# Hybrid two-layer block, FP32 by split products: block products by seven in the first feed-forward matrix instead of the second

## The chip, the cores and the metric

The kernel runs on one core of a Trainium2 chip. The metric is the device time of one execution in microseconds (us). Three runs of the kernel before stand beside one profiled execution, which the hardware recorded instruction by instruction. The engines are TensorE (PE, with PEld for its weight loads), VectorE (DVE), ScalarE (ACT), GpSimd (POOL) and SyncE (SP), which issues the DMAs.

## The reference

A sequence of 256 tokens of width 1024 goes through two layers. Each layer is feed-forward, mixer, feed-forward, each followed by a residual and a layer norm. The mixer of layer 0 is a hybrid of a gated delta rule and a state-space scan, that of layer 1 a sparse attention; neither is touched by the change. The part that matters, four times in all:

```python
D_MODEL, SEQ, D_FF = 1024, 256, 2816

def swiglu(x, w_in, w_out):
    gate, up = jnp.split(x @ w_in, 2, axis=-1)      # w_in 1024 x 5632
    return (jax.nn.silu(gate) * up) @ w_out         # w_out 2816 x 1024

h = layer_norm(DEEPNORM_ALPHA * h + 0.5 * swiglu(h, ffn_w_in[layer, 0], ffn_w_out[layer, 0]),
               ln_g[layer, 0], ln_b[layer, 0])
```

All is float32.

## The kernel before

**Split products.** Every float32 operand of the large products is split into a high part and a low part (`split`, `hard_split`): ACT copies it rounded (`whi`, `fhi`, `g`), DVE subtracts that from the source (`wlo`, `flo`). A product is then three: high by high, high by low, low by high (`mm3`). Each weight is loaded once from HBM, in raw tiles of 128 x 2048 (1 MB, four buffers, `RAW = 4`), split into halves of 128 x 1024, and used once, since all 256 tokens fit in one pass. Everything in fast memory besides the raw tiles, the tokens and small constants comes from one pool of 36 tiles of 128 x 1024 (`m4`), shared by streams with quotas: "W" for split weights, "G" for gated activations, "F" for sums, "L" for the residual.

**A feed-forward** (`ffn`) goes through its 2816 features in 11 steps of 256. Steps 0 and 1 compute tokens by features and transpose the result (`pair_weights`, `proj_tok`). Steps 2 to 10 are ordinary: for each 128 features, `proj_two` multiplies 8 blocks of the weights' high part by the tokens' high and low parts side by side (8 matmuls of 512 columns), and 8 of the low part by the high one (8 of 256), for the gate and again for the up half; `add_two` adds the two sides, ACT takes silu, DVE multiplies, and the gated block is split into `g`. In the program such matmuls read `ps<-x,whi` and `ps<-x,wlo`. The second matrix adds each block of 128 features into four PSUM banks (`acc`, two token blocks by two column halves): 12 matmuls of 512 columns, `out_mm`.

**Seven for eight, before.** For steps 4 to 7 (`SEVEN = (4, 8)`) the second matrix is done by a scheme with seven block products in place of eight (a Strassen-Winograd form). Two blocks of 128 features and two token blocks give the sums of activations (`token_forms`, tiles `F`, `fhi`, `flo`), two feature blocks and two column halves those of weights (`weight_forms`, tiles `t13`, `t24`), and seven products of 128 x 128 by 128 x 512, each three matmuls, go into banks which are combined at the end into the residual (`put`, tiles `u`). The gated blocks of steps 8 to 10 then go through `out_mm` for the first token block, and, while its layer norm runs on DVE, for the second (`late`).

**The order.** Nothing is issued as written. `Plan` records all operations; `order` schedules them as a list with prices and latencies written in the class, program order as priority, tiles handed out when a buffer is free, and the program emits what results: one fixed queue for each engine. In a feed-forward the copies to high parts are fixed to ACT (`self.hard`). Since every operation is issued from one place, all lines of the profile read L540, and groups are told apart by the names of tiles.

Of the kernel before, what the change touches and what calls it, by code (L numbers as in the profile page):

```python
# [18 lines left out]
P = 128  # L19
# [14 lines left out]

QUOTAS = {"M": None, "D": None, "F": None, "S": (8, 8), "Z": (4, 4), "L": (4, 4), "G": (20, 20), "P": (5, 5), "Q": (5, 5), "W": (12, 24)}

# [14 lines left out]
SEVEN = (4, 8)  # L51
# [512 lines left out]
class K:  # L564
# [3 lines left out]
    def __init__(self, plan, ins, caps):  # L568
        self.nc = self.plan = plan
        self.i = ins  # L570
        self.caps = caps
        self.strand = ""
        self.most, self.hard = 0, False
        self.consts()
# [24 lines left out]
    def m4(self, n, name, stream="M", dtype=F32):  # L599
        quota = (12, self.most) if stream == "W" and self.most else QUOTAS[stream]  # L600
        return self.plan.tile("m4", [P, 1024], dtype, name, stream=stream, quota=quota)[:, :n]
# [40 lines left out]
    def split(self, hi, lo, src):  # L642

        self.copy(hi, src)
        self.nc.vector.tensor_tensor(lo, src, hi.bitcast(F32), OP.subtract)


    def unit(self, srcs, parts):

        raw = self.plan.tile("raw", [P, 2048], F32, "raw", stream="W")  # L650
        for dst, src in srcs:
            self.nc.sync.dma_start(dst(raw), src)
        out = []
        for f in parts:
            v = f(raw)
            n = int(v.ids.size)
# [5 lines left out]
            (self.hard_split if self.hard else self.split)(hi, lo, v)  # L662
            out.append((hi, lo))
        return out
# [56 lines left out]
    def hard_split(self, hi, lo, src):  # L721

        self.nc.scalar.activation(hi, src, AF.Copy)
        self.nc.vector.tensor_tensor(lo, src, hi.bitcast(F32), OP.subtract)

    def weight_forms(self, w, k0):

        nc, V = self.nc, self.nc.vector
        raw = self.plan.tile("raw", [P, 2048], F32, "raw", stream="W")
        nc.sync.dma_start(H3(raw, 2), w[:, k0:k0 + 2, 0:D])  # L730
        q = raw.rearrange("p (k c n) -> p k c n", k=2, c=2)
        new = lambda name, dt=F32R: H3(self.m4(1024, name, "W", dt), 2)
        h1, l1 = new("whi"), new("wlo")
        self.hard_split(h1, l1, q[:, :, 0])
        t13, t24 = new("t13", F32), new("t24", F32)
        V.tensor_tensor(t13, q[:, 0], q[:, :, 1], OP.add)
        b22 = new("whi")
        self.hard_split(b22[:, 0], b22[:, 1], q[:, 1, 1])
        h2, l2 = new("whi"), new("wlo")
        self.hard_split(h2, l2, t13)  # L740
        V.tensor_tensor(t24[:, 0], t13[:, 0], q[:, 1, 1], OP.add)
        V.tensor_tensor(t24[:, 1], t24[:, 0], q[:, 1, 0], OP.add)
        h3, l3 = new("whi"), new("wlo")
        self.hard_split(h3, l3, t24)
        return dict(b11=(h1[:, 0], l1[:, 0]), b21=(h1[:, 1], l1[:, 1]), b22=(b22[:, 0], b22[:, 1]),
                    t1=(h2[:, 0], l2[:, 0]), t3=(h2[:, 1], l2[:, 1]), t2=(h3[:, 0], l3[:, 0]), t4=(h3[:, 1], l3[:, 1]))

    def token_forms(self, F):

        V = self.nc.vector  # L750
        n = lambda j: F[:, j]
        V.tensor_tensor(n(4), n(1), n(3), OP.subtract)
        V.tensor_tensor(n(1), n(0), n(1), OP.subtract)
        V.tensor_tensor(n(5), n(4), n(0), OP.subtract)
        V.tensor_tensor(n(6), n(2), n(5), OP.add)
        hi, lo = (self.m4(1024, name, "G", F32R).rearrange("p (j t) -> p j t", j=8)[:, :7] for name in ("fhi", "flo"))
        self.hard_split(hi, lo, F[:, :7])
        f = lambda j: (hi[:, j], lo[:, j])
        return dict(b11=f(0), b21=f(2), b22=f(6), t1=f(4), t3=f(1), t2=f(5), t4=f(3))
# [13 lines left out]

    def transpose_half(self, x, b, h, q, scale=None, c0=None):
# [6 lines left out]
        src = pt.rearrange("p (k t) -> p k t", k=4)  # L781
        if scale is not None:
# [192 lines left out]
    def ffn(self, l, j, x, then, last=False):  # L975
# [13 lines left out]

        def out_mm(b, f, g, wo, cols=range(2)):  # L990
            for c in cols:
                cs = slice(c * 512, (c + 1) * 512)
                bs = slice(b * P, (b + 1) * P)
                self.mm3(acc[b][c], (g[0][:, bs], g[1][:, bs]), (wo[0][:, cs], wo[1][:, cs]), f == 0,
                         f == NF - 1 - (ENDS if last and b == 1 and c == 1 else 0))
# [26 lines left out]
        forms = {}  # L1022

        def flush(keep):
            while len(todo) > keep:
                f, g, wo = todo.pop(0)
                out_mm(0, f, g, wo)
                out_mm(1, f, g, wo)
        for s in range(NT, DFF // 256):
            self.most = min(24, 31 - 2 * (s - SEVEN[0]) if s < SEVEN[1] else 21 + SEVEN[1] - s)  # L1030
# [6 lines left out]
            if s == NT + 4:  # L1037
                self.mark = len(self.plan.ops) - 1
            seven = SEVEN[0] <= s < SEVEN[1]
            if seven:  # L1040
                F = self.m4(1024, "F", "F").rearrange("p (j t) -> p j t", j=8)
            for e in range(2):
                if e and s < SEVEN[0]:
# [6 lines left out]
                if seven:  # L1050
                    nc.vector.tensor_tensor(F[:, 2 * e:2 * e + 2].rearrange("p a t -> p (a t)"), sg, up, OP.mult)
                else:
                    nc.vector.tensor_tensor(sg, sg, up, OP.mult)
                    g = gts[f] = gtiles(f)
                    self.hard_split(g[0], g[1], sg)
                if s >= SEVEN[0]:
                    flush(0)
                elif e == 0:
# [6 lines left out]
            if seven:  # L1065
                forms[s] = self.token_forms(F)
        flush(0)
        banks = {n: self.bank(tag) for n, tag in (("b11", "mp"), ("t1", "mp"), ("t3", "ps"), ("t2", "ps"))}
        banks.update(b21=acc[0][0], b22=acc[0][1], t4=acc[1][0])
        for s in range(*SEVEN):  # L1070
            self.most = min(24, 20 + max(0, s - SEVEN[0] - 1) * 2)
            w = self.weight_forms(w_out, 2 * s)
            for n in ("b21", "b11", "b22", "t1", "t3", "t2", "t4"):
                own = n in ("b11", "t1", "t3", "t2")
                self.mm3(banks[n], forms[s][n], w[n], own and s == SEVEN[0], own and s == SEVEN[1] - 1)
        tail = []
        self.most = 0
        for s in range(SEVEN[1], NF // 2):
            wo = self.unit_rows(w_out, 2 * s, 2, 0, D)
            tail += [(2 * s + e, gts[2 * s + e], wo[e]) for e in range(2)]  # L1080
        V = nc.vector
        u = [H3(self.m4(1024, "u", "F"), 2) for n in range(2)]
        side = lambda b, c: self.ah[b][:, c * 512:(c + 1) * 512]

        def put(b, c, k, src):
            V.scalar_tensor_tensor(side(b, c), src, k, side(b, c), OP.mult, OP.add)
        p1, us, vs, xs = u[0][:, 0], u[0][:, 1], u[1][:, 0], u[1][:, 1]
        nc.scalar.activation(p1, banks["b11"], AF.Copy)
        V.tensor_tensor(us, banks["t2"], p1, OP.add)
        V.tensor_tensor(vs, banks["t1"], us, OP.subtract)  # L1090
        put(0, 0, 0.5, p1)
        put(0, 1, 0.5, vs)
        for f, g, wo in tail:
            out_mm(0, f, g, wo)
            late.append((f, g, wo))
        self.hard = False
        then(0, acc)
        V.tensor_tensor(us, banks["t3"], us, OP.add)
        V.tensor_tensor(xs, banks["t1"], us, OP.subtract)
        put(1, 0, 0.5, us)  # L1100
        put(1, 1, 0.5, xs)
# [976 lines left out]
    def run(self, stages):  # L2078
# [3 lines left out]
        x = self.new_x()  # L2082
# [23 lines left out]
        for n, (kind, l, j, idx) in enumerate(stages):  # L2106
# [4 lines left out]
            def then(b, acc, s, state=state, last=last, l=l, idx=idx):  # L2111
                if b == 0:
                    state['x'] = None if last else self.new_x()
                    state['gb'] = self.ln_params(l, idx)
# [55 lines left out]
```

## Time and profile before

| | us |
|---|---|
| three runs | 2806.3, 1109.99, 1111.8; median 1111.8 |
| profiled execution, its own time | 1110.35 |
| its span, first to last instruction | 1108.6 |
| PE busy (share of span) | 1093.8 (99%) |
| DVE busy | 915.2 (83%) |
| ACT busy | 638.5 (58%) |
| DMA, mean | 178 GB/s |

By the two layer norms that end each stage (their small GpSimd power instruction marks them), the four feed-forwards take the first 197 us, 435 to 619, 619 to 801 and 926 to 1108.6; the hybrid mixer lies between 197 and 435, the sparse attention between 801 and 926. A row of the profile names output and inputs (`wlo<-raw,whi`), shape, count, busy time and the mean of one in ns, then the idle time ahead of it and what ended it. The duration that a row gives to one instruction overlaps that of the next on the same engine, so distances between starts are what an engine can sustain.

### The profile page before, as it was taken

Reading aid. Unit: us, or ns where it says so; the run is one execution under the profiler, and the core shown is the slowest. Engines: PE = TensorE matmul, PEld = TensorE weight load, DVE = VectorE, ACT = ScalarE, POOL = GpSimd, SP = SyncE. Lnnn points to the kernel's source line nnn. Section 1 sums busy time; section 2 is a strip of 40 time slices with the busy share of each in tenths; the row PEclk is TensorE's granted clock in tenths of the full one; section 3 lists DMA queues with packets and bytes.
Section 4 is the critical chain, followed back from the end, with each engine's and each line's share of the span. In section 5 each row is a group of like instructions: output and inputs, shape, how many; then the busy total and the mean of one; then the engine's idle time right before and its main releaser. Section 6 shows DMA issues by size and latency. Waiting matters only on the chain. (4 is left out here: it accounts for less than half of the span.)

```text
span 1108.6 us, 16690 instructions
## 1 busy us (share of the span) xinstructions
PE 1093.8 (99%) x6497; PEld 936.2 (84%) x6497; DVE 915.2 (83%) x1515; ACT 638.5 (58%) x1091; POOL 56.2 (5%) x103
## 2 busy tenths in 40 slices
PE   9999999999999999999999999999999999999997
PEld 7888888898999888888888888888887778888885
DVE  6956889899979999766789966789978979657887
ACT  5846555278736454554666645656466776555560
POOL 1000000012001320000000000000000100000000
PEclk9999999999999999999999999999999999999999
DMA  9965437641932266844538766443836237664431
GB/s 335 318 223 171 152 116 241 218 133 44 268 114 79 113 215 211 293 154 156 182 104 267 251 219 196 152 152 121 260 107 243 77 114 259 223 202 149 155 114 38
DMA packets 147848, 197.86 MB, mean 178 GB/s; under 512 B 9373, under 2 KB 122682, under 8 KB 147770
## 3 DMA queue, kind: packets, MB, share of 16 engines
q1 hardware_dynamic: 147770, 196.80, 54.0%
q8 instruction: 51, 0.84, 0.3%
q14 instruction: 27, 0.22, 0.1%
HBM read 194.04 MB, written 1.05 MB: 176 GB/s over the span
## 5 line engine op out<-in xcount | busy, mean ns | idle before, releaser
L540 DVE TENSOR_TENSOR wlo<-raw,whi 128x1024 fp32r<-128x1024 f32 (+3 forms) x335 | 396.9, 1205 | 51.3 <-ACT whi L540 50.2
L540 PE MATMUL ps<-x,whi 128*128 128x512 f32 (+2 forms) x1584 | 370.2, 364 | 2.0 <-ACT cv L540 1.1
L540 ACT ACTIVATE whi<-raw 128x1024 fp32r<-128x1024 f32 (+2 forms) x329 | 324.0, 1019 | 45.3 <-DMA raw<-in_ffn_w_in_dram 22.3
L540 PEld LDWEIGHTS ps<-x,whi 128*128 128x128 f32 (+1 forms) x1584 | 275.8, 188 | 44.2 <-ACT cv L540 3.0
L540 PE MATMUL ps<-x,wlo 128*128 128x256 f32 x1368 | 222.7, 283 | 0.0
L540 PEld LDWEIGHTS ps<-x,wlo 128*128 128x128 f32 x1368 | 197.7, 190 | 11.3
L540 ACT ACTIVATE sg<-ps 128x256 f32<-128x256 f32 x156 | 59.5, 382 | 157.7 <-PE ps L540 157.1
L540 PE MATMUL acc<-whi,g 128*128 128x512 f32 x442 | 140.6, 391 | 0.0
L540 PE MATMUL ps<-whi,x 128*128 128x512 f32 (+1 forms) x480 | 129.3, 385 | 0.9 <-DVE x L540 0.9
L540 DVE TENSOR_TENSOR sg<-ps,sg 128x256 f32<-128x256 f32 (+1 forms) x158 | 67.0, 424 | 60.8 <-ACT sg L540 58.2
L540 PEld LDWEIGHTS ps<-whi,x 128*128 128x128 f32 x480 | 85.6, 188 | 16.8 <-DVE x L540 1.7
L540 PEld LDWEIGHTS acc<-whi,g 128*128 128x128 f32 x442 | 83.0, 188 | 16.7
L540 PE MATMUL acc<-wlo,g 128*128 128x512 f32 x221 | 86.6, 392 | 0.0
L540 PE MATMUL acc<-whi,x 128*128 128x512 f32 x224 | 73.5, 404 | 0.5 <-ACT x L540 0.3
L540 PE MATMUL ps<-wlo,x 128*128 128x512 f32 (+1 forms) x240 | 67.6, 382 | 0.0
L540 DVE TENSOR_TENSOR wlo<-t,whi 128x1024 fp32r<-128x1024 f32 x32 | 39.1, 1221 | 13.8 <-ACT whi L540 13.8
L540 PEld LDWEIGHTS acc<-whi,x 128*128 128x128 f32 x224 | 41.5, 189 | 9.7 <-DVE x L540 0.7
L540 PEld LDWEIGHTS ps<-wlo,x 128*128 128x128 f32 x240 | 43.5, 188 | 7.1
L540 POOL TENSOR_TENSOR lnve<-lnve,mhalf 128x1 f32<-128x1 f32 x12 | 11.5, 956 | 737.9 <-DVE lnve L540 737.9
L540 PEld LDWEIGHTS acc<-wlo,g 128*128 128x128 f32 x221 | 41.6, 188 | 7.8
L540 ACT ACTIVATE whi<-t 128x1024 fp32r<-128x1024 f32 x32 | 33.9, 1059 | 23.7 <-DVE t L540 23.0
L540 ACT ACTIVATE sg<-sg 128x256 f32<-128x256 f32 x72 | 29.9, 415 | 28.3 <-DVE sg L540 28.1
(282 smaller groups left out, 1371.3 us busy)
## 6 DMA issues: line engine op xcount, KB each, us to landing
raw<-in_ffn_w_in_dram SPq DMA_DIRECT2D x72, 1024.0 KB, 5.2
raw<-in_ffn_w_out_dram SPq DMA_DIRECT2D x44, 1024.0 KB, 5.0
raw<-in_hyb_w_in_dram SPq DMA_DIRECT2D x20, 1024.0 KB, 5.3
raw<-in_ffn_w_in_dram SPq DMA_DIRECT2D x30, 512.0 KB, 5.0
raw<-in_hyb_w_out_dram SPq DMA_DIRECT2D x8, 1024.0 KB, 5.1
raw<-in_nsa_w_in_dram SPq DMA_DIRECT2D x5, 1024.0 KB, 5.2
raw<-in_nsa_cmp_w_dram SPq DMA_DIRECT2D x4, 1024.0 KB, 5.4
raw<-in_nsa_w_out_dram SPq DMA_DIRECT2D x4, 1024.0 KB, 7.8
```

The lines of the kernel that those rows point to most:

```text
L540: r = getattr(getattr(nc, eng), fn)(*[res(a) for a in args], **{k: res(a) for k, a in kw.items()})
```

## The change

The second matrix becomes ordinary everywhere. In the first matrix, three chunks of 512 features (features 1280 to 2815, steps 5 to 10 of before) are done by the seven-product scheme: the blocks are two token blocks by two halves of the 1024 inputs, and two input halves by gate and up. Each of the seven products is 128 tokens by 512 inputs by 512 features: 12 matmuls with the tokens stationary and weights of 512 columns moving (`mp<-whi,x`, `mp<-whi,fhi`, `mp<-wlo,fhi`). Token sums are made once for each feed-forward from unsplit copies of the tokens (`X`), weight sums in place in the four raw tiles of a chunk. The result is tokens by features, so eight transposes follow. The chunks are interleaved with the remaining ordinary steps 2 to 4 by the table `WIDE`, letters standing for products.

```diff
-QUOTAS = {... "G": (20, 20), ...}
+QUOTAS = {... "G": (6, 6), ...}
-SEVEN = (4, 8)
+WIDE = ("abcd", "efg", "abcd", "efg", "abcdefg", "")
...
+    def token_forms(self, x):
+        V = self.nc.vector
+        (a11, a21), (a12, a22) = ((X[:, 0], X[:, 1]) for X in x[3])
+        V.tensor_tensor(a22, a21, a22, OP.subtract)
+        V.tensor_tensor(a21, a11, a21, OP.subtract)
+        V.tensor_tensor(a11, a22, a11, OP.subtract)
+        V.tensor_tensor(a12, a12, a11, OP.add)
...
+        return dict(a=part(0, 0), b=s1, c=part(0, 4), d=s2, e=s3, f=part(1, 4), g=s4)
+
+    def wide(self, w_in, c0, forms, gout, then):
...
+        def load(k0, c):
+            raw = self.plan.tile("raw", [P, 2048], F32, "raw", stream="W")
+            nc.sync.dma_start(h4(raw), w_in[:, k0:k0 + 4, c:c + 512])
+            return raw
...
+        def add(out, a, b):
+            for e in range(2):
+                cs = slice(e * 1024, e * 1024 + 1024)
+                V.tensor_tensor(out[:, cs], a[:, cs], b[:, cs], OP.add)
...
+            for e, (wh, wl) in enumerate(w):
+                for k in range(2):
+                    n = 2 * e + k
+                    mm(bank, ah[:, n], wh[:, k], start=start and n == 0)
+                    mm(bank, al[:, n], wh[:, k])
+                for k in range(2):
+                    n = 2 * e + k
+                    mm(bank, ah[:, n], wl[:, k], stop=n == 3)
+
+        b11 = load(0, c0)
+        w = halves(b11)
+        b12 = load(0, DFF + c0)
+        p, q = self.bank("mp"), self.bank("mp")
...
+        product(p, "a", w, True)
+        nc.scalar.activation(s, p, AF.Copy)
+        yield
+        add(b11, b11, b12)
+        product(q, "b", halves(b11), True)
+        yield
+        b21 = load(4, c0)
+        product(p, "c", halves(b21), False)
+        nc.scalar.activation(sg, p, AF.Silu)
+        yield
+        b22 = load(4, DFF + c0)
+        add(b11, b11, b22)
+        product(p, "d", halves(b11), True)
+        V.tensor_tensor(u, p, s, OP.add)
+        yield
+        add(b12, b12, b22)
+        product(p, "e", halves(b12), False)
+        V.tensor_tensor(v, p, s, OP.add)
+        V.tensor_tensor(v, q, v, OP.subtract)
+        yield
+        add(b11, b11, b21)
+        product(p, "f", halves(b11), False)
+        V.tensor_tensor(s, p, s, OP.add)
+        nc.scalar.activation(s, s, AF.Silu)
+        yield
+        product(q, "g", halves(b22), False)
+        V.tensor_tensor(u, q, u, OP.subtract)
+        V.tensor_tensor(sg, sg, u, OP.mult)
+        V.tensor_tensor(s, s, v, OP.mult)
...  (two groups of four transposes into "mp", then split into gh, gl)
...
-            seven = SEVEN[0] <= s < SEVEN[1]
...
+                if s == NT and e == 0:
+                    forms = self.token_forms(x)
+                for name in next(turns):
+                    if name == "a":
+                        next_wide()
+                    next(chunks[-1])
...
-        for s in range(*SEVEN):
-            w = self.weight_forms(w_out, 2 * s)
-            for n in ("b21", "b11", "b22", "t1", "t3", "t2", "t4"):
-                self.mm3(banks[n], forms[s][n], w[n], ...)
```

How the change moves instructions shows in three places of the second feed-forward (435 us on in the trace of before). Rows are those of the emitted program.

On PE, in before, steps 4 to 10 are `ps` products of the gate and up halves one after the other (`x_4489` are the tokens):

```order
L540 MATMUL ps_5295<-x_4489,whi_5023 128x512 x8
L540 MATMUL ps_5295<-x_4489,wlo_5033 128x256 x8
L540 MATMUL ps_5320<-x_4489,whi_5065 128x512 x8
L540 MATMUL ps_5320<-x_4489,wlo_5077 128x256 x8
L540 MATMUL ps_5352<-x_4489,whi_5050 128x512 x8
L540 MATMUL ps_5352<-x_4489,wlo_5058 128x256 x8
```

On PE now, in the first chunk, the third product (`c` in the code) and the beginning of the fourth (`d`), which share a bank (`mp_4728`; `x_4370` are the tokens, `fhi_4526` a sum of tokens), with a part of an ordinary `ps` product between them:

```order
L540 MATMUL mp_4728<-whi_4657,x_4370 128x512 x4
L540 MATMUL mp_4728<-wlo_4681,x_4370 128x512 x2
L540 MATMUL mp_4728<-whi_4675,x_4370 128x512 x4
L540 MATMUL mp_4728<-wlo_4692,x_4370 128x512 x2
L540 MATMUL ps_4775<-x_4370,whi_4402 128x512 x4
L540 MATMUL mp_4728<-whi_4711,fhi_4526 128x512
```

Ordinary products, which stood in a row, now fill the places where a bank is read between two products of a chunk.

On DVE, in before, in steps 4 to 7 of the same feed-forward, subtractions of 128 x 1024 for the weights stand among small operations of the gated product and its sums:

```order
L540 TENSOR_TENSOR sg_5488<-ps_5461,sg_5488 128x256
L540 TENSOR_TENSOR wlo_5499<-raw_5287,whi_5484 128x1024
L540 TENSOR_TENSOR sg_5488<-ps_5486,sg_5488 128x256
L540 TENSOR_TENSOR F_5473<-sg_5488 128x256
L540 TENSOR_TENSOR F_5473<-F_5473 128x128
L540 TENSOR_TENSOR wlo_5524<-raw_5287,whi_5509 128x1024
```

On DVE now, in the first chunk (`raw_4436`, `raw_4487`, `raw_4568`, `raw_4592` are its four raw tiles, `raw_4762` the next rows of the second matrix):

```order
L540 TENSOR_TENSOR raw_4436<-raw_4436,raw_4592 128x1024 x2
L540 TENSOR_TENSOR raw_4487<-raw_4487,raw_4592 128x1024
L540 TENSOR_TENSOR wlo_4725<-raw_4436,whi_4711 128x1024
L540 TENSOR_TENSOR wlo_4733<-raw_4436,whi_4719 128x1024
L540 TENSOR_TENSOR raw_4487<-raw_4487,raw_4592 128x1024
L540 TENSOR_TENSOR raw_4436<-raw_4436,raw_4568 128x1024 x2
L540 TENSOR_TENSOR wlo_4799<-raw_4762,whi_4790 128x1024
L540 TENSOR_TENSOR su_4809<-mp_4728,su_4746 128x512
```

The sums in place stand between the subtractions, and the last reader of `raw_4568` is followed at once by the first user of `raw_4762`.

On SP, which issues the loads, in before:

```order
L540 DMA raw_4718<-in_ffn_w_in_dram 128x8x256
L540 DMA raw_4738<-in_ffn_w_in_dram 128x8x256
L540 DMA raw_4786<-in_ffn_w_in_dram 128x8x256
L540 DMA raw_4828<-in_ffn_w_in_dram 128x8x256
L540 DMA raw_4867<-in_ffn_w_in_dram 128x8x256
```

And now, at the first chunk:

```order
L540 DMA raw_4436<-in_ffn_w_in_dram 128x4x512
L540 DMA raw_4487<-in_ffn_w_in_dram 128x4x512
L540 DMA raw_4568<-in_ffn_w_in_dram 128x4x512
L540 DMA raw_4592<-in_ffn_w_in_dram 128x4x512
L540 DMA raw_4762<-in_ffn_w_out_dram 128x2x1024
```

Before, each raw tile was held for the two subtractions that read it. Now the four tiles of a chunk take all four raw buffers until their sums are done, so the load of `raw_4762` stands behind the release of `raw_4568`.

More of the change, by code (lines that the diff above doesn't have):

```diff
@@ L572, in __init__ @@
         self.strand = ""
-        self.most, self.hard = 0, False
+        self.hard = False
         self.consts()
@@ L599, in m4 @@
     def m4(self, n, name, stream="M", dtype=F32):
-        quota = (12, self.most) if stream == "W" and self.most else QUOTAS[stream]
+        quota = QUOTAS[stream]
         return self.plan.tile("m4", [P, 1024], dtype, name, stream=stream, quota=quota)[:, :n]
@@ L642, in split @@
     def split(self, hi, lo, src):
-        self.copy(hi, src)
+        if self.hard:
+            self.nc.scalar.activation(hi, src, AF.Copy)
+        else:
+            self.copy(hi, src)
         self.nc.vector.tensor_tensor(lo, src, hi.bitcast(F32), OP.subtract)
@@ L719, in first_weights @@
         return out
[L721 to L726, printed above, removed]
-        nc, V = self.nc, self.nc.vector
[L729 to L759, printed above, removed]
+    def token_forms(self, x):
[5 more added lines that the diff above has]
+        V.tensor_tensor(a12, a12, a11, OP.add)
+        out = []
+        for X in x[3]:
+            hi, lo = (self.m4(1024, n, "F", F32R).rearrange("p (b k t) -> p b k t", b=2, k=4) for n in ("fhi", "flo"))
+            self.split(*(t.rearrange("p b k t -> p (b k t)") for t in (hi, lo, X)))
+            out += [(hi[:, b], lo[:, b]) for b in range(2)]
+        s2, s3, s4, s1 = out
+        part = lambda b, k0: tuple(x[e][:, k0:k0 + 4, b, :] for e in range(2))
+        return dict(a=part(0, 0), b=s1, c=part(0, 4), d=s2, e=s3, f=part(1, 4), g=s4)
@@ L772, in new_x, with new_forms @@
         return [t[:, :, 0], t[:, :, 1], t]
+    def new_forms(self, x):
+        x.append([self.m4(1024, f"X{q}", "F").rearrange("p (b k t) -> p b k t", b=2, k=4) for q in range(2)])
+        return x
     def transpose_half(self, x, b, h, q, scale=None, c0=None):
@@ L993, in out_mm @@
                 bs = slice(b * P, (b + 1) * P)
-                self.mm3(acc[b][c], (g[0][:, bs], g[1][:, bs]), (wo[0][:, cs], wo[1][:, cs]), f == 0,
-                         f == NF - 1 - (ENDS if last and b == 1 and c == 1 else 0))
+                n = count[b, c] = count.get((b, c), 0) + 1
+                self.mm3(acc[b][c], (g[0][:, bs], g[1][:, bs]), (wo[0][:, cs], wo[1][:, cs]), n == 1,
+                         n == NF - (ENDS if last and b == 1 and c == 1 else 0))
         gts = {}
@@ L1021, in ffn, with flush, next_wide, ready @@
         late = []
-        forms = {}
-        def flush(keep):
-            while len(todo) > keep:
+        def flush(keep, most=NF):
+            while len(todo) > keep and most:
+                most -= 1
                 f, g, wo = todo.pop(0)
                 out_mm(0, f, g, wo)
-                out_mm(1, f, g, wo)
-        for s in range(NT, DFF // 256):
-            self.most = min(24, 31 - 2 * (s - SEVEN[0]) if s < SEVEN[1] else 21 + SEVEN[1] - s)
+                if count[0, 0] > NF - self.LAG - (3 if last else 0):
+                    late.append((f, g, wo))
+                else:
+                    out_mm(1, f, g, wo)
+        steps = NF // 2 - 2 * sum("a" in turn for turn in WIDE)
+        chunks = []
+        def next_wide():
+            n = len(chunks)
+            f0 = 2 * steps + 4 * n
+            gout = [self.m4(1024, name, "G", F32R).rearrange("p (f t) -> p f t", f=4) for name in ("gh", "gl")]
+            def ready():
+                for s in range(2):
+                    wo = self.unit_rows(w_out, f0 + 2 * s, 2, 0, D)
+                    todo.extend((f0 + 2 * s + e, tuple(t[:, 2 * s + e, :] for t in gout), wo[e]) for e in range(2))
+            chunks.append(self.wide(w_in, f0 * P, forms, gout, ready))
+        turns = iter(WIDE)
+        for s in range(NT, steps):
             wg = self.unit_cols(w_in, s * 256, 256)
@@ L2081, in run @@
         self.first = True
-        x = self.new_x()
+        x = self.new_forms(self.new_x())
         warm = self.bank("acc")
@@ L2109, in run, with then @@
             state = {}
-            def then(b, acc, s, state=state, last=last, l=l, idx=idx):
+            def then(b, acc, s, state=state, last=last, l=l, idx=idx, n=n):
                 if b == 0:
                     state['x'] = None if last else self.new_x()
+                    if not last and stages[n + 1][0] == 'ffn':
+                        self.new_forms(state['x'])
                     state['gb'] = self.ln_params(l, idx)
```

77 lines of the change are left out of this document (32 added, 45 removed).

## The prediction

> **What bounds the kernel now.** I read the page's busy shares first, then the idle time of the PE groups, then a table of stretches through one feed-forward, then the chain that ended last.
>
> ```profile
> span 1108.6 us, 16690 instructions
> ...
> PE 1093.8 (99%) x6497; PEld 936.2 (84%) x6497; DVE 915.2 (83%) x1515; ACT 638.5 (58%) x1091; POOL 56.2 (5%) x103
> ...
> L540 PE MATMUL ps<-x,whi 128*128 128x512 f32 (+2 forms) x1584 | 370.2, 364 | 2.0 <-ACT cv L540 1.1
> ```
>
> PE is busy for 99% of the span, and its costliest group waited 2.0 us in 1584 matmuls. A busy PE could still be a slow one, so its pace has to be read from stretches in which nothing else happens:
>
> ```profile
> 978.90 2.75 PE acc L540 x12
> ...
> 992.67 72.60 PE ps L540 x416
> ...
> 1083.66 14.96 PE acc L540 x66
> ```
>
> Second-matrix matmuls of 512 columns follow each other at 2.75/12 = 0.229 or 14.96/66 = 0.227 us. The 416 `ps` matmuls are 26 groups of sixteen (eight of 512 and eight of 256 columns): 72.60/26 = 2.79 us for a group, so 0.229 for 512 columns leave 0.120 for 256. PE's time in the feed-forwards is thus the number of columns it is given. DVE is second. The nine stretches of the second feed-forward show where it has room:
>
> ```profile
> 435.00:619.00 184.00, 183.57 (x954) 156.86 (x954) 145.77 (x211) 105.55 (x160) 1.93 (x3) 1.00 0.58 192
> ...
> 475.00:497.00 22.00, 22.00 (x120) 19.05 (x119) 13.18 (x17) 12.07 (x19) 0.00 (x0) 1.00 0.55 178
> 497.00:519.00 22.00, 22.00 (x120) 19.06 (x119) 13.94 (x21) 10.74 (x17) 0.00 (x0) 1.00 0.48 157
> ...
> 585.00:607.00 22.00, 22.00 (x99) 18.23 (x98) 20.81 (x26) 14.50 (x16) 0.00 (x0) 1.00 0.87 283
> 607.00:619.00 12.00, 11.57 (x56) 9.25 (x55) 12.00 (x19) 6.45 (x10) 1.18 (x2) 1.00 0.64 187
> ```
>
> The columns are the stretch, its length, then PE, PEld, DVE, ACT and POOL with instructions, the granted clock, and DMA. PE is full throughout. DVE does 13 to 14 us in 22 in the middle and is full around the layer norm at the end. So PE's work counts in full, and DVE has 38 us of room in 184.
>
> **PE's part of the change.** All counts are of the emitted programs. Each of three chunks in four feed-forwards replaces two ordinary steps, which are eight groups of sixteen: 96 groups go, 96 x 2.79 = 268.0 us. In come 12 x 7 products of 12 matmuls of 512 columns, 1008 x 0.227 to 0.229 = 228.5 to 230.9 us. The price is that of the `acc` rows, which have the same shape.
>
> Each chunk also adds eight transposes of 128 x 128. The trace has such transposes between matmuls:
>
> ```profile
> 437.10 0.60 PE L540 MATMUL mp<-ident,h 128*128 128x128 f32 x4
> 437.46 0.48 PE L540 MATMUL ps<-whi,x 128*128 128x512 f32 x1
> 437.77 0.60 PE L540 MATMUL mp<-ident,h 128*128 128x128 f32 x4
> ```
>
> From one group of four to the next, 0.67 us with one 512-column matmul in it: 0.44 for four, 0.11 each, and 96 x 0.11 = 10.6 us. The second matrix loses its scheme: in four steps 96 matmuls in place of 84, 48 more in all, 48 x 0.228 = 10.9 us.
>
> PE's sum: 268.0 - 229.7 - 10.6 - 10.9 = **16.8 us less** (15.6 to 18.0), 4.2 for each feed-forward. Taken from the profiled execution's own 1110.35, which lies 1.4 below the median of 1111.8, that gives 1093.5 if PE never waits.
>
> **DVE's part.** Its pace is read from distances between starts:
>
> ```profile
> 571.37 0.42 DVE L540 TENSOR_TENSOR sg<-ps,sg 128x256 f32<-128x256 f32 x1
> 571.70 1.22 DVE L540 TENSOR_TENSOR wlo<-raw,whi 128x1024 fp32r<-128x1024 f32 x1
> ...
> 587.81 6.89 DVE L540 TENSOR_TENSOR wlo<-raw,whi 128x1024 fp32r<-128x1024 f32 x6
> 594.62 0.69 DVE L540 TENSOR_TENSOR u<-ps,u 128x512 f32<-128x512 f32 x1
> 595.22 0.68 DVE L540 SCALAR_TENSOR_TENSOR h<-u,h 128x512 f32<-128x512 f32 x1
> ```
>
> Six of 1024 elements take 594.62 - 587.81 = 6.81, 1.135 each; one of 512 takes 0.60, one of 256 0.33. For each feed-forward the change adds 24 sums of weights, 14 more subtractions and 2 for token sums, all of 1024, and 31 operations of 512: 40 x 1.135 + 31 x 0.60 = 64.0 us. It removes 8 of 1024 or 896, 20 of 512, 40 of 256, and 16 of 128 (0.2 each, an estimate from the step between those sizes): 8.5 + 12.0 + 13.2 + 3.2 = 36.9. Net +27: DVE's 145.8 become 173 in a stage in which PE's 183.6 become 179.4. DVE goes from 79% to 96% of PE. ACT gains 12 copies of 1024 and 14 operations of 512 and loses 40 of 256; even at 1.06 for each one added (the copy of 1024 in the rows further down) and nothing for those removed that is 28 us, 134 of 179, so it is not the bound.
>
> The Trainium skill, "VectorE: DVE Perf Modes", section "The DRAIN you can't avoid", speaks against this: it says that the next operation does not start before the pipeline of the last has emptied, and its formula in the section on the errata makes 1.224 us of 1024 elements, which is the duration in the row of 571.70. By that rule DVE would need some 11 us more in each feed-forward than by the distances. The row of 587.81 disagrees with it, 1.135 from start to start.
>
> **The new wait.** The four raw tiles of a chunk fill all four buffers. The next rows of the second matrix can be loaded only when the third tile is released, and in DVE's queue their first subtraction stands right behind the last reader (in the second chunk, one 512 and one 256 operation stand between, 0.9 us). Everything behind it on DVE waits, the reads of the product banks included, and PE waits for those. The length of such a hole, from the nearest rows:
>
> ```profile
> 828.06 2.38 SPq L540 DMA_DIRECT2D raw<-in_nsa_w_in_dram  x2
> 836.47 4.30 SPq L540 DMA_DIRECT2D raw<-in_nsa_w_out_dram  x4
> ...
> 833.35 1.06 ACT L540 ACTIVATE whi<-raw 128x1024 fp32r<-128x1024 f32 x1 [5.71 <-DMA raw<-in_nsa_w_in_dram]
> 842.51 1.06 ACT L540 ACTIVATE whi<-raw 128x1024 fp32r<-128x1024 f32 x1 [1.69 <-DMA raw<-in_nsa_w_out_dram]
> ...
> 441.92 1.06 ACT L540 ACTIVATE whi<-raw 128x1024 fp32r<-128x1024 f32 x1
> ...
> 443.01 1.23 DVE L540 TENSOR_TENSOR wlo<-raw,whi 128x1024 fp32r<-128x1024 f32 x1 [0.53 <-ACT whi L540]
> ```
>
> Issue to the ACT copy 5.3 (828.06 to 833.35) or 6.0 (836.47 to 842.51), copy to subtraction 1.1: 6.4 to 7.1 us. There are two such holes in each feed-forward; ahead of the third chunk's rows 8.6 us of other DVE work stand, which covers it.
>
> Whether PE feels the holes is a race of two queues. I counted both between points where PE uses what DVE made, in the second feed-forward, with the prices above. From step 1's last transposes to step 3's first weights: PE 181 x 0.228 + 40 x 0.12 + 10 x 0.11 = 47.2; DVE 28 x 1.135 + 7 x 0.60 + 9 x 0.33 = 39.0, with the hole 45.4 to 46.1. To the same place of the next chunk: PE 203 x 0.228 + 32 x 0.12 + 8 x 0.11 = 51.0; DVE 33 x 1.135 + 11 x 0.60 + 8 x 0.33 = 46.7, with the hole less 0.9 52.2 to 52.9. To the transposes of the third: PE 35.4; DVE 25 x 1.135 + 7 x 0.60 + 4 x 0.33 = 33.9. Together PE 133.6, DVE 131.5 to 132.9. PE stays ahead as the later queue, by 0.7 to 2.1 us, 1% of the stretch: **the two engines finish side by side**, and anything else that DVE waits for lands on PE. In before such waits exist and cost nothing, since DVE has room:
>
> ```profile
> DVE wlo L540 <- ACT whi L540: 64.0, 56, 6.1
> ```
>
> 56 waits of 1.1 us on average. At least 0 of that reaches PE; at most, in the forecast's own case, the 4.2 us gained. I take 1.5 us for each feed-forward, about one such wait and some at the layer norm, where the products that run beside it (second token block) shrink from 36 matmuls, 8.2 us, to 30, 6.9. The first feed-forward starts with no lead of DVE over PE, so 1 us more there. Loss 4 x 1.5 + 1 = 7.
>
> **Forecast:** 1110.35 - 16.8 + 7 = **1100 us**, 1% faster.
>
> **The rivals.**
>
> *The gain is eaten.* DVE is late by 4 us or more in each feed-forward, and PE waits for it. For: the 1% above. Against: DVE was full from 585 to 619 and PE lost 0.43 us there. Two or three of the 1.1 us waits would do: 1110.35 - 16.8 + 4 x 4.5 = 1112, between 1108 and 1122.
>
> *The holes stand on PE's path.* Where DVE has no lead when the third tile is released, the whole hole falls on PE: eight holes of 6.4, 51 us, 1145. The sign turns when a hole costs PE 2.1 us (16.8/8), and 2% slower takes 4.9. For: the four buffers are certainly full. Against: the first stretch's 47.2 against 39.0 shows a lead of 8 us being made ahead of the first hole.
>
> *DVE runs at the durations.* If sums in place on raw tiles, a form that no row of before has, went at 1.22 from start to start as all others too, the three stretches' 86 operations of 1024 and 46 smaller ones, 0.085 each, add 11 us of DVE and 10 of PE in each: 1134. Against: the row of 587.81. This is the rule of the page named above.
>
> *Nothing is lost.* 1093 and as low as 1090, if ordinary products fill every gap.
>
> That the program does not do what it says is excluded by the counts, which agree with the scheme.
>
> **How the numbers follow.** Chances: forecast (1094 to 1108) 0.60; eaten 0.22; holes on PE 0.06; durations 0.02; nothing lost 0.08; something not thought of on the fast side 0.02. The predicted time is the forecast's. The range takes in forecast, nothing lost and eaten: 1090 to 1122, with 0.1 left out. 2% of 1110, 22 us, is about what a measurement can tell from no change here. Faster than that needs more than PE's whole gain: 0.03. Slower comes from the holes and the durations: 0.08. Within: 0.89.
>
> **What would show it.** PE: 96 `ps` groups fewer, `mp<-whi,x` and `mp<-wlo,fhi` at 0.227 to 0.229 between starts, and PE's idle time up by some 7 us, inside the feed-forwards. DVE: busy about 915 + 4 x 27 = 1023. ACT: waits of about 5 us for the second matrix's loads, two in each feed-forward, and DVE holes of 6 to 7 there. Wrong would be: matmuls of the chunks slower than 0.23; sums in place at 1.2 from start to start; PE idle by 4 us or more in a feed-forward at `mp` products or at the next ordinary step.

## The result, and the profile after

Before: 1111.2 us median, with a fourth run. After: 1103.5 us (1102.5 to 1104.5). The ratio is 0.9937, 95% interval 0.9922 to 0.9952: 0.7% faster, well inside the 2% that count as no change here. The forecast was 1100, the range 1090 to 1122. The profiled executions stand at 1110.35 before and 1103.07 after, a gain of 7.3 us where 16.8 - 7 = 9.8 were forecast (the sum was 1100.55, put as 1100).

The page of the changed kernel, span, busy shares and two of the costliest groups (line, engine, operation, tiles, shape, count, busy us, mean ns of one, idle time ahead and what ended most of it):

```profile
span 1101.3 us, 15842 instructions
...
PE 1081.5 (98%) x6113; PEld 907.4 (82%) x6113; DVE 999.4 (91%) x1452; ACT 663.9 (60%) x1046; POOL 69.9 (6%) x103
...
L540 PE MATMUL ps<-x,whi 128*128 128x256 f32 (+2 forms) x816 | 184.7, 339 | 4.7 <-ACT whi L540 3.3
...
L540 DVE TENSOR_TENSOR raw<-raw,raw 128x1024 f32<-128x1024 f32 x96 | 114.0, 1223 | 0.0
```

PE has 12.3 us less busy time, and 19.8 us of the span are not busy in place of 14.8. The `ps` group has 768 matmuls fewer, which are the 512-column half of the 96 groups that went; its idle time rose from 2.0 to 4.7 us, now put down to `ACT whi`. DVE's busy time rose by 84 us, not by the 108 of the forecast.

The stretches of two feed-forwards after the change (stretch, length, PE, PEld, DVE, ACT, POOL, clock, DMA):

```profile
0.00:197.40 197.40, 192.16 (x887) 156.76 (x888) 178.46 (x212) 124.20 (x165) 4.49 (x21) 1.00 0.65 222
436.10:617.60 181.50, 179.84 (x859) 149.65 (x858) 167.96 (x198) 110.78 (x147) 1.90 (x3) 1.00 0.58 197
```

The second feed-forward, 184.0 before, is 2.5 us shorter, and DVE has 13.5 us of it free, not 6.4. The first one takes 197.4 us and took 197.2: it gained nothing.

A page puts a wait into PE's busy time when it is shorter than what the modelled end of a matmul (0.39 us after its start) adds to the distance of 0.227. So I worked out a ledger from the trace instead: for every PE instruction the distance to the next start; up to the usual distance of its shape (0.227 for 512 columns, 0.120 for 256, 0.109 for 128, and so on) it is work, and the rest is loss, which is taken as a net sum within a feed-forward. All in us:

| kernel | PE's work, whole program | loss: first 34 us | rest of the first feed-forward | second | third | fourth | loss in all four |
|---|---|---|---|---|---|---|---|
| before | 1085.0 | 5.1 | 2.2 | 1.5 | 1.4 | 0.7 | 10.9 |
| after | 1068.8 | 7.4 | 5.2 | 3.0 | 3.4 | 1.5 | 20.5 |
| no chunks | 1095.9 | 5.1 | 0.6 | 0.8 | 0.7 | 0.7 | 7.9 |
| two chunks | 1077.8 | 7.6 | 4.3 | 0.7 | 0.8 | 2.4 | 15.8 |
| narrow sums | 1068.8 | 6.0 | 4.8 | 2.3 | 3.2 | 1.2 | 17.5 |
| 34 tiles | 1068.9 | 7.2 | 5.3 | 1.5 | 5.3 | 1.6 | 20.9 |
| 34 tiles, 5 raw | 1068.8 | 7.8 | 4.3 | 1.2 | 0.7 | 0.7 | 14.7 |
| 5 raw, forms first | 1068.8 | 5.3 | 4.0 | 1.2 | 0.7 | 0.6 | 11.8 |
| 5 raw, forms first, order for 5 | 1068.7 | 5.7 | 0.7 | 0.6 | 0.9 | 0.6 | 8.5 |
| four chunks | 1059.6 | 5.0 | 16.7 | 10.4 | 6.2 | 6.6 | 44.9 |

Work fell by 16.2 us (16.8 forecast). Loss rose by 9.6 in the feed-forwards (7 forecast) and fell by 0.6 in the two other stages: 16.2 - 9.6 + 0.6 = 7.2, the 7.3 of the spans but for rounding. What the runs had to settle is what PE waits for in those 9.6.

The waits of PE by name (who, waited for whom, us in total, times, longest) after the change:

```profile
PE ps L540 <- ACT whi L540: 3.3, 5, 1.3
PE mp L540 <- DVE vg L540: 1.3, 1, 1.3
PE mp L540 <- DVE h L540: 1.1, 1, 1.1
...
PE acc L540 <- DVE x L540: 0.9, 1, 0.9
```

The first of these was not there before. Five times PE stands at an ordinary step behind a chunk, because the high part of a weight has not been copied. In four of the five ACT had itself waited for the load of that weight (the fifth, 0.2 us, stood behind a wait of ACT for a product bank). The longest of them in the timeline (start, length, engine, operation, count, idle time ahead and releaser), first three loads that SP issued before it, then PE and ACT:

```profile
669.32 6.61 SPq L540 DMA_DIRECT2D raw<-in_ffn_w_in_dram  x3
```

```profile
679.06 0.39 PE L540 MATMUL acc<-whi,g 128*128 128x512 f32 x1
...
679.62 2.01 ACT L540 ACTIVATE whi<-raw 128x1024 fp32r<-128x1024 f32 x2 [2.67 <-DMA raw<-in_ffn_w_in_dram]
...
680.73 0.97 PE L540 MATMUL ps<-x,whi 128*128 128x512 f32 x3 [1.28 <-ACT whi L540]
```

PE waits 1.28 us for ACT; ACT had waited 2.67 us for the transfer, the second of the three, issued at 672.73. The product banks have no part in it, and DVE has one only as the engine that gives raw tiles back. Why the transfer was late is seen in the waits of SP's own queue from 668 to 680 us:

```profile
SPq L540 <- DVE wlo L540: 16.2, 5, 5.9
```

The five waits follow one another from 666.8 to 684.7 us (the first and the last reach out of the window): each load stands until a `wlo`, the last reader of a raw tile, is done. The load in question stood 3.0 us, and ACT could start 6.9 us after its issue; the median from issue to landing is 5.3. The four raw buffers go round between a chunk's tiles, the rows of the second matrix and the next step's columns, and each load can be issued only when an older tile has been split.

### The profile page after: what moved, and what is told of

Same layout as the page of the kernel before. It is cut to its first block, busy times and chain, and to the rows that moved or that the text cites. A ratio compares the mean times of both kernels' runs of the same rounds, so it can differ in the third digit from the quotient of the medians.

```text
span 1101.3 us, 15842 instructions
## 1 busy us (share of the span) xinstructions
PE 1081.5 (98%) x6113; PEld 907.4 (82%) x6113; DVE 999.4 (91%) x1452; ACT 663.9 (60%) x1046; POOL 69.9 (6%) x103
## 5 line engine op out<-in xcount | busy, mean ns | idle before, releaser
L540 DVE TENSOR_TENSOR wlo<-raw,whi 128x1024 fp32r<-128x1024 f32 (+2 forms) x423 | 500.6, 1210 | 13.7 <-ACT whi L540 12.6
L540 ACT ACTIVATE whi<-raw 128x1024 fp32r<-128x1024 f32 (+2 forms) x403 | 405.0, 1047 | 118.9 <-DVE raw L540 55.3
L540 PE MATMUL ps<-x,whi 128*128 128x256 f32 (+2 forms) x816 | 184.7, 339 | 4.7 <-ACT whi L540 3.3
L540 PEld LDWEIGHTS ps<-x,whi 128*128 128x128 f32 (+1 forms) x816 | 137.1, 188 | 23.6 <-ACT whi L540 5.7
L540 PE MATMUL ps<-x,wlo 128*128 128x256 f32 (+1 forms) x600 | 116.4, 284 | 0.0
L540 DVE TENSOR_TENSOR raw<-raw,raw 128x1024 f32<-128x1024 f32 x96 | 114.0, 1223 | 0.0
L540 PEld LDWEIGHTS ps<-x,wlo 128*128 128x128 f32 (+1 forms) x600 | 93.4, 189 | 4.2
L540 PE MATMUL mp<-whi,x 128*128 128x512 f32 x288 | 77.1, 389 | 0.0
L540 PE MATMUL mp<-whi,fhi 128*128 128x512 f32 x192 | 75.2, 392 | 0.0
L540 PE MATMUL mp<-whi,flo 128*128 128x512 f32 x192 | 74.8, 390 | 0.0
```

The costliest lines, as they stand in the source:

```text
L540: r = getattr(getattr(nc, eng), fn)(*[res(a) for a in args], **{k: res(a) for k, a in kw.items()})
```

## The experiments

Theory **DVE**, that of the prediction: DVE is almost as long as PE, and what it waits for lands on PE. Theory **loads**: four raw buffers are too few once a chunk holds four tiles at once, and the weights behind it come late, however fast DVE is. Theory **order at the seams**: the exact copies of the tokens stand ahead of the forms that PE needs next.

**No chunks.**

```diff
-WIDE = ("abcd", "efg", "abcd", "efg", "abcdefg", "")
+WIDE = ("",) * 18
-                    forms = self.token_forms(x)
+                    pass
```

(`new_forms` returns at once.)

> No chunks at all: every step of the first matrix is ordinary and the second matrix stays ordinary, so both schemes are gone (the exact copies and sums of the tokens too). All theories: PE has 48 more 512-column matmuls than before the change, 48 x 0.228 = 10.9 us, and DVE has more room than in any other version, so 1111.2 + 10.9 = 1122 (1120 to 1124). Then three chunks in each feed-forward are worth 1122 - 1103.5 = 18.5 of the 27.7 us that PE's counts give. A time under 1118 would say that the scheme for the second matrix, which the change gave up, did not gain what its counts say, and that the change's loss stands there and not in the chunks.

Measured 1118.2 (1118.1 to 1118.7), ratio to before 1.0067 (1.0052 to 1.0082): below the 1120 that all theories gave as the least, though not below 1118. The ledger says why: PE's work is 10.9 us more than before, as counted, but the loss is 3.0 us less (7.9 against 10.9). So the kernel with the scheme for the second matrix had some 3 us of waits that go with it. In profiled executions the three chunks take 1116.9 - 1101.3 = 15.6 us off the span, of 27.1 us of work.

**Two chunks.**

```diff
-WIDE = ("abcd", "efg", "abcd", "efg", "abcdefg", "")
+WIDE = ("abcd", "efg", "abcd", "efg") + ("",) * 6
```

> Two chunks in each feed-forward in place of three; by PE's counts 9.2 us more work than the changed kernel (4 x 2.31), which is 1094.3 + 9.2 = 1103.5 if nothing is lost. Theory DVE (the loss comes from DVE being nearly as long as PE): two chunks leave DVE some 10 us more room in a feed-forward, only the start of the program loses its 2.4 us, so 1106 (1105 to 1107). Theory loads (the loss comes from four raw buffers, once behind every chunk): two thirds of some 7 us and 2.4 at the start, 1110.5 (1109 to 1112).

Measured 1108.0, ratio 0.9978 (0.9963 to 0.9992), with single runs from 1103.7 to 1112.7. It lies between the two forecasts and spreads over both: it tells nothing apart.

**Narrow sums.**

```diff
-                cs = slice(e * 1024, e * 1024 + 1024)
+                cs = slice(e * 1024, e * 1024 + 64)
                 V.tensor_tensor(out[:, cs], a[:, cs], b[:, cs], OP.add)
```

(A second edit, two lines in the pricing, keeps the price of a whole sum.)

> The changed kernel, with the 96 sums of weights in place cut to 64 columns each, so most of each sum is left out; they are priced for the order as if whole, so that every engine's queue is in the same order. DVE loses 24 x (1.135 - 0.136) = 24 us in each feed-forward. Theory DVE: the waits of PE inside the feed-forwards go, what is left is the start of the program, 1103.5 - 6 = 1097 (1096 to 1099). Theory loads: PE's waits for ACT's copies of the next ordinary step's weights come from transfers that can't be issued while chunk and second matrix hold all four raw buffers; DVE's release of these is earlier by some us, but the waits do not go as a whole: 1101 (1099 to 1103). Neither theory changes the 2.4 us at the start.

Measured 1100.0 (1099.7 to 1101.9), 3.5 us less than the changed kernel, inside the interval of the loads and outside that of DVE. The waits (of PE, then of DVE; the second edit moved the line to L542):

```profile
PE ps L542 <- ACT whi L542: 3.0, 5, 0.9
...
PE mp L542 <- DVE vg L542: 1.3, 1, 1.3
```

```profile
L542 DVE TENSOR_TENSOR su<-mp,su 128x512 f32<-128x512 f32 x36 | 24.7, 686 | 62.3 <-PE mp L542 62.1
```

The same row of the changed kernel:

```profile
L540 DVE TENSOR_TENSOR su<-mp,su 128x512 f32<-128x512 f32 x36 | 24.8, 688 | 20.6 <-PE mp L540 20.3
```

DVE now stands 62.1 us for the product banks, in place of 20.3: it is far ahead of PE. PE's waits for `ACT whi` are still five, 3.0 us of 3.3. In the ledger the loss fell by 3.0 of 20.5. But 1.4 of that lie in the first 34 us, and the first sum of a chunk starts at 42.3 us in the changed kernel, so they are not the sums' doing (the section on the start, below, says what differs there). That leaves 1.6, half of it at one layer norm, where PE's wait for `DVE h` fell from 1.1 to 0.3. **Theory DVE falls** as the main cause: 96 us less work on DVE returned 3.5 at the most.

**Forms first, at every seam.**

```diff
-        if len(x) > 3:
-            nc.scalar.activation(x[3][q][:, b], src, AF.Copy)
         ...
         self.split(x[0][:, q * 4:q * 4 + 4, b, :], x[1][:, q * 4:q * 4 + 4, b, :], src)
+        if len(x) > 3:
+            nc.scalar.activation(x[3][q][:, b], src, AF.Copy)
```

> The same work; the exact copy of the transposed tokens (X, which only the sums for the chunks read) is recorded behind the two forms that the next matmuls read (x high and low part), not ahead of them. Theory order at the seams: the first 32 us lost 2.4 us since ACT copied X out of the product bank before DVE and ACT had made x, and the layer norms lost some tenths each in the same way, so 1100.5 (1099.5 to 1101.5). Theories DVE and loads alone: no change, 1103.5 (1102.5 to 1104.5).

Measured 1102.1 (1101.0 to 1103.7), between the two. The start did get its 2.8 us back (loss in the first 34 us 7.4 to 4.6); at the later seams PE's waits for `DVE h` rose from 1.1 to 3.1.

**34 tiles, then 34 tiles and five raw buffers.**

```diff
-RAW, M4 = 4, 36
+RAW, M4 = 4, 34
```

> Control for the next run: the changed kernel with 34 in place of 36 buffers for the 4 KB tiles, which sets space free for a fifth raw buffer; the order is made again for 34. Every theory: within 2 us of the changed kernel's 1103.5 (1102.5 to 1106), and again some 4 us in which PE waits for ACT's copies of the weights of the ordinary step behind a chunk.

Measured 1103.4 (1103.1 to 1103.7). Then, with the order already made, one buffer more:

```diff
-        pools[tag] = (ctx.enter_context(tc.tile_pool(name="t_" + tag, bufs=n, **kw)), n)
+        pools[tag] = (ctx.enter_context(tc.tile_pool(name="t_" + tag, bufs=n + (tag == "raw"), **kw)), n)
```

> As the control with 34, its order unchanged on every engine and queue, but with five raw buffers in place of four when it runs. Theory loads: the loads of the ordinary step behind each chunk no longer wait for a raw buffer that the rows of the second matrix hold, PE's waits of some 4.2 us for ACT's copies go, so 4 us less than the control, 1099.5 (1098.5 to 1101). Rival, distance in the order: PE waits at these places since the copies stand too late in ACT's own queue, behind copies for other tiles; then 1 us less at most. Rival DVE, which the narrow sums have already made small: the control's time.

Measured **1096.1** (1095.0 to 1097.5), ratio to before 0.987 (0.9855 to 0.9886): 7.25 us less than the control, with the same instructions in the same order on every engine. The profiled spans differ by 6.3, the losses of the ledger by 6.2. The waits of the control:

```profile
ACT whi L540 <- DMA raw<-in_ffn_w_in_dram: 26.3, 23, 2.6
...
PE ps L540 <- ACT whi L540: 3.5, 4, 1.1
PE mp L540 <- DVE h L540: 1.7, 1, 1.7
PE mp L540 <- DVE vg L540: 1.3, 1, 1.3
```

and with five raw buffers:

```profile
ACT whi L540 <- DMA raw<-in_ffn_w_in_dram: 4.6, 4, 1.9
...
PE mp L540 <- DVE vg L540: 1.3, 1, 1.3
PE acc L540 <- POOL ones L540: 1.1, 1, 1.1
```

ACT's waits for the first matrix fall from 26.3 us in 23 waits to 4.6 in four. `PE ps <- ACT whi` is gone, and so is `PE mp <- DVE h`, at the layer norm that ends the third feed-forward. There, too, a late load stood at the beginning, one of the sparse attention's weights. In the control ACT waits for it, and DVE for ACT's copy of a gated block behind it:

```profile
780.26 0.91 ACT L540 ACTIVATE whi<-raw 128x840 fp32r<-128x840 f32 x1 [5.84 <-DMA raw<-in_nsa_w_in_dram]
...
781.51 0.42 DVE L540 TENSOR_TENSOR g<-sg,g 128x256 fp32r<-128x256 f32 x1 [2.34 <-ACT g L540]
```

With five buffers ACT waits 2.68 us for that load, and DVE not at all. **Theory loads is shown**: one buffer more, and nothing else, takes the waits away. Its size was not forecast: 1096.1 is below its 1098.5 to 1101, since it counted only the waits that carried the copy's name.

**Rows later**, with four raw buffers. The load of a chunk's rows waits until the next step's columns have been recorded:

```diff
-            chunks.append(self.wide(w_in, f0 * P, forms, gout, ready))
+            chunks.append(self.wide(w_in, f0 * P, forms, gout, lambda: owed.append(ready)))
         ...
             wu = self.unit_cols(w_in, DFF + s * 256, 256)
+            while owed:
+                owed.pop(0)()
```

> The changed kernel with four raw buffers; the load and split of a chunk's rows of the second matrix are recorded behind the weights of the next ordinary step, not ahead of them, so that the wait for a raw buffer falls on the rows, which PE needs later. Theory loads: 3 to 4 us less, 1100 (1099 to 1101.5). Rival: the wait only changes its place, since the same four buffers serve the same tiles, 1103.5 (1102 to 1106), and PE waits for rows of the second matrix instead.

Measured 1107.0 (1105.5 to 1109.9), 3.5 us slower than the changed kernel and above both forecasts. PE's first waits:

```profile
PE mp L540 <- DVE P L540: 2.4, 1, 2.4
PE ps L540 <- ACT x L540: 2.2, 1, 2.2
PE acc L540 <- ACT whi L540: 1.7, 2, 1.3
PE mp L540 <- DVE vg L540: 1.4, 2, 0.8
```

`ps <- ACT whi` is gone here as well, but `acc <- ACT whi`, the rows of the second matrix, stands in its place. In the ledger the four feed-forwards lose 19.9 us, against 20.5 in the changed kernel: with four buffers this order moved the waits and did not remove them. The extra time is not theirs. The profiled run (1109.05, above the median) loses 5.8 us more than the changed kernel in the sparse attention, which the edit does not touch but whose order is made anew with everything else; the `DVE P` wait stands there, at 822 us.

**Forms first, at the start alone.** As above, under `early = len(self.plan.ops) < 400`.

> The exact copy behind the two forms, as in the run before, but in the first feed-forward alone; the seams at the layer norms keep the changed kernel's order. Theory order at the seams: the first 34 us get the 2.8 us back that the run with all seams showed there (7.4 us of PE lost there against 4.6), and the later seams stay: 1100.7 (1100 to 1101.5). Rival: what the start gains is lost at the next wait for loads, which then comes with no more slack, 1102 to 1103.5.

Measured 1101.9, single runs from 1099.8 to 1103.2. The profiled one is the 1099.8, and its first 34 us lose 5.8 where 7.4 were lost. The spread is as wide as the effect; by the median some 1.5 us.

**The kernel before, with five raw buffers** (34 tiles, the same two lines edited).

> The kernel before the change, ordered for 34 of the 4 KB tiles and run with five raw buffers. Theory loads, as a thing of the chunks (which hold four raw tiles at once): before the change a raw tile is held for one unit alone, PE waited for no copy in the feed-forwards, so next to nothing changes, 1110 (1108.5 to 1111.5). Rival: the fifth buffer helps any version by the same 7 us, 1104; then it says nothing on the change.

Measured 1108.2 (1108.1 to 1108.9), ratio to before 0.9978 (0.9969 to 0.9987), just below the interval of theory loads and far from the rival's 1104. So 2.5 us are not a thing of the chunks (whether they come from the buffer or from the order for 34 tiles was not tried), and some 4.8 of the 7.25 are. Five buffers against five, the change is worth 1108.2 - 1096.1 = 12.1 of the 16.2 us.

**Five raw buffers and forms first at the start**, and the same with the order made for five (`RAW, M4 = 5, 34`).

> The changed kernel, ordered for 34 tiles, run with five raw buffers, and with the exact copy behind the two forms in the first feed-forward. If the two losses are separate they add: 1096.1 - 1.6 (by the medians of the run with the forms alone) to 1096.1 - 3.3 (by its profiled run), 1092.8 to 1094.5. Rival, one slack for both: the start's gain is taken up by a later wait, 1096.

> As the run with five raw buffers and the forms first, but with the order itself made for five raw buffers. If the order made for four still carries waits of its own (loads issued late in the queue), 1 to 2 us less than that run, 1092 (1090.5 to 1094); if an order is as good as another within what such orders differ by, the same to 2 us more.

Measured 1094.7 (1094.6 to 1095.2), ratio to before 0.9856 (0.9841 to 0.9871), and 1095.1 (1094.0 to 1095.6). The first gains 1.4 more, close to the smaller of the two gains and just outside the interval (1094.5); that speaks for separate losses, as far as 1.4 us can. The second is the same within its runs, but not in its parts: in the ledger its feed-forwards lose 3.3 us less, and its sparse attention, ordered anew, loses 2.5 more. These are the fastest versions, 1.4% below before and 0.8% below the change as made.

**Four chunks**, five raw buffers, forms first at the start.

```diff
-WIDE = ("abcd", "efg", "abcd", "efg", "abcdefg", "")
+WIDE = ("abcdefgabcdefg", "abcdefgabcdefg")
```

(The number of ordinary steps follows, and `self.mark` is set in the last of them.)

> Four chunks in each feed-forward (the last possible: three ordinary steps are left), five raw buffers, the forms first at the start. By PE's counts 9.2 us less than with three chunks, 1084.5. DVE's own time in a feed-forward (stage less idle time, third stage) was 123 us with none, 154 with two, 168 with three chunks, so 182 with four, against PE's 178.4 - 2.3 = 176: theory DVE bound: each feed-forward goes to 184 or more, 1094 + 4 x 5 = 1114 (1104 to 1122). If the time stays under 1095, DVE is not what bounds even there.

Measured 1124.9 (1123.3 to 1125.6), ratio 1.0123 (1.0106 to 1.014), 30 us above three chunks, though PE's work is 9.2 us less, as counted. Two of its stretches and PE's first waits:

```profile
443.10:625.60 182.50, 177.41 (x805) 144.50 (x804) 181.24 (x203) 114.59 (x141) 1.91 (x2) 0.98 0.54 193
625.60:808.90 183.30, 180.36 (x837) 147.99 (x836) 180.88 (x222) 107.42 (x134) 4.22 (x4) 1.00 0.50 174
```

```profile
PE mp L540 <- DVE su L540: 7.4, 5, 2.2
PE mp L540 <- DVE h L540: 5.8, 2, 3.5
PE acc L540 <- ACT gh L540: 3.0, 3, 1.6
```

DVE is busy for 181.2 of 182.5 us, and PE waits for `DVE su` and `DVE h`. This is what a feed-forward bound by DVE looks like, and the changed kernel, with 13.5 us free on DVE, does not look like it. The time is 11 us above the 1114 that DVE's 182 us gave, and above the interval. Up to some 9 of these 11 us go with the clock: the trace records half the clock in five stretches, 20.4 us in all (from 145.5, 196.7, 620.0, 879.4 and 1101.3 us on), in which matmuls of 512 columns follow each other at 0.427 in place of 0.227 us, and PE loses about 9 us there between matmuls with no idle time ahead. Four of the five begin within 2 us of the end of a wait of 1.5 to 3.5 us for DVE. The changed kernel's profile has no such stretch between 10.3 us and its last matmuls.

## Why the prediction was right or wrong, by its steps

**PE's work: right.** 16.8 forecast, 16.2 in the ledger. The prices held, in the chunk's own matmuls:

```profile
468.15 1.07 PE L540 MATMUL mp<-whi,x 128*128 128x512 f32 x4
469.06 0.62 PE L540 MATMUL mp<-wlo,x 128*128 128x512 f32 x2
...
473.14 0.62 PE L540 MATMUL mp<-wlo,fhi 128*128 128x512 f32 x2
473.59 0.39 PE L540 MATMUL mp<-whi,x 128*128 128x512 f32 x1
```

From 468.15 to 473.59 are 24 matmuls (rows left out included): 0.2267 each. The second matrix's 10.9 comes out as counted: the kernel without chunks has 10.9 more work than before. Only 7.3 to 8.3 of it show in time, since the kernel with the scheme lost 3 us more.

**The loss: 7 forecast, 9.6 measured; the amount near, the mechanism wrong.** The failed step is "the two engines finish side by side", that is, the race of the two queues. It had PE as the later queue by only 0.7 to 2.1 us over a feed-forward's three chunks, so that whatever DVE waits for lands on PE. Here is what happened, in the second feed-forward on DVE:

```profile
469.97 3.49 DVE L540 TENSOR_TENSOR raw<-raw,raw 128x1024 f32<-128x1024 f32 x3
479.44 1.23 DVE L540 TENSOR_TENSOR wlo<-raw,whi 128x1024 fp32r<-128x1024 f32 x1 [5.98 <-ACT whi L540]
480.58 0.69 DVE L540 TENSOR_TENSOR su<-mp,su 128x512 f32<-128x512 f32 x1
```

and at the same place of the fourth, on ACT and on DVE:

```profile
961.06 0.60 ACT L540 ACTIVATE vg<-mp 128x512 f32<-128x512 f32 x1 [4.78 <-PE mp L540]
964.53 2.01 ACT L540 ACTIVATE whi<-raw 128x1024 fp32r<-128x1024 f32 x2 [2.87 <-DMA raw<-in_ffn_w_out_dram]
...
964.84 0.69 DVE L540 TENSOR_TENSOR su<-mp,su 128x512 f32<-128x512 f32 x1 [5.51 <-PE mp L540]
```

The forecast hole of 6.4 to 7.1 is there once, 5.98 us; in the third and fourth feed-forward DVE stands 5.66 and 5.51 us at the same place, but for PE's product bank: it is that far ahead, and the late rows cost nothing. Nor is any PE wait put down to `wlo` or the banks there. The shortage of raw buffers, which the prediction named, bit one use later: at the columns of the next ordinary step, on a path DMA, ACT, PE on which DVE matters as the engine that gives tiles back. The prediction had looked for what waits on DVE's queue, and had not followed the freed buffers through SP's queue to the next load. That 7 came near 9.6 was luck. Priced were 2.5 us for the first feed-forward and 1.5 for each other one, as waits behind DVE; the losses rose by 5.3, 1.5, 2.0 and 0.8, and the fifth buffer, which leaves DVE's work as it is, took 6.2 away. The rest is in the main the start and the `vg` wait below.

**The start: mis-sized.** One us more was allowed for the first feed-forward; its first 34 us lost 2.3 more than before, the rest of it 3.0, and all its gain went. With the exact copies ahead of the forms, the second group of transposes of the tokens stands later in PE's queue, and nothing fills PE's wait for the first tokens, where before four matmuls of ones stood. Rows of after, then of before:

```profile
5.72 2.48 PE L540 MATMUL acc<-whi,x 128*128 128x512 f32 x4 [0.88 <-DVE x L540]
...
10.68 0.60 PE L540 MATMUL mp<-ident,h 128*128 128x128 f32 x4
```

```profile
4.64 1.75 PE L540 MATMUL acc<-ones 128*128 128x256 f32 x4
...
7.29 0.60 PE L540 MATMUL mp<-ident,h 128*128 128x128 f32 x4
```

The four matmuls of 5.72 follow each other at 0.57 us on average (to 8.00), in place of 0.227: PE is not yet at its pace. The trace's record of the full clock begins at 10.3 us after the change and at 6.1 before, and 1.5 of the 2.3 us are lost between matmuls with no idle time ahead. This differs between profiles whose PE starts with the same instructions: from 9.6 and 10.6 us on in the two kernels with 34 tiles (7.2 and 7.8 lost), from 4.5 with the narrow sums (6.0 lost). So of the start's loss a part is the order and a part is when the full clock came, and one profile of each cannot divide them.

With the forms first the start got 1.6 to 2.8 us back, and in the three profiles with three chunks and the changed kernel's order elsewhere the full clock came at 4.7 to 4.9 us. The `vg` wait of 1.3 us, at 173 us, stayed where the order stayed; with the order made for five buffers the rest of the first feed-forward loses 0.7 us in all. It was not taken apart further.

**DVE's busy time: mis-sized by 24 us, its work not.** The counts of DVE's operations in the traces are as forecast, but for 11 copies outside the forecast that the order gave to ACT this time (2 of 1024 elements, 2 of 512, 3 of 256, 4 of 128: some 5 us by the prediction's prices). Busy time counts each operation's whole 1.22 us when idle time follows, and 1.135 when the next one starts under its tail. Before, 422 of DVE's operations followed idle time, after the change 223: 199 tails of 0.085 us, 17 of the missing 24, were already in the 915.2 and fell away. With the 11 copies that is 22 of the 24. So the base was too high for a sum at distances between starts, and DVE had twice the room that I gave it.

**The rivals.** The distance of 1.135 holds for sums in place as well: 3.49 for three of them (the row of 469.97) is 1.135 from start to start, so that the rule of the Trainium skill, "VectorE: DVE Perf Modes", section "The DRAIN you can't avoid", as the prediction cites it, does not describe this form either; the section itself adds that an operation which is not held starts earlier. Gain eaten, holes on PE and nothing lost did not come; the first was 8 us off. With a fifth raw buffer "nothing lost" almost came true: 1096.1, and 1094.7 with the forms first, against 1093.5, though 2.5 us of that came to the kernel before as well.

## What to carry to other kernels

When a change holds several buffers of a pool at once, follow each freed buffer to the load that takes it next, and on to the engine that needs that load: here the wait came out there, and not where the buffers were taken. To tell a shortage of buffers from a shortage of an engine, keep the order of all queues, add one buffer in one run and take the engine's work away in another. When a run is slower or faster, look first in which stage: an order that is made anew can lose in a stage that the edit does not touch. Sum distances between starts against distances between starts: a busy time that holds the tails of lone operations makes an engine look fuller than it is.

## What was not expected of the hardware

The DMA issues of the page with five raw buffers (count, KB each, median us from issue to landing):

```profile
raw<-in_ffn_w_in_dram SPq DMA_DIRECT2D x72, 1024.0 KB, 5.4
raw<-in_ffn_w_out_dram SPq DMA_DIRECT2D x44, 1024.0 KB, 4.9
```

In the control, with four, they took 5.1 and 4.9: the transfers are not faster, one more can be under way. That this was worth 7.25 us of 1103, while 96 us less work on an engine busy for 91% of the span was worth 3.5 at the most, I had not expected.
